# Parameter rows on ScalarE's queue, all of x loaded ahead of the embedding product, first six weight loads behind x

## The chip, the cores and the metric

The kernel runs on one core of one Trainium2 chip. The core has five engines that run side by side and wait for one another through semaphores: TensorE (PE in the profile; its weight loads are PEld), VectorE (DVE), ScalarE (ACT), GpSimd (POOL) and SyncE (SP). Data moves between HBM and the on-chip memory by DMA, over 16 DMA engines. The metric is the device time of one execution in microseconds (us); lower is better.

## The reference

One decoder layer over 1024 tokens of width 1024, all in float32:

```
u  = rms_norm(x, ln_g)
z  = u @ w_in                       # 1024 x 7168, split into val, glu, gate, q, f, i, g
y_conv = conformer_conv_branch(val, glu, gate, ...)   # GLU, causal conv of width 31, norm, swish, projection
y_hgrn = hgrn2_branch(q, f, i, g, ...)                # gated linear recurrence, 8 heads
h  = x + concat(y_conv, y_hgrn) @ w_out
pe = p @ w_pp                       # p is 1024 x 256
h  = h + sigmoid(rms_norm(h, pe_norm_g) @ w_pg) * pe
out = rms_norm(h, final_g)
```

Nine small parameter tables (the convolution's 31 taps, biases, norm gains, two rows of logits) have one value per channel.

## The kernel before

Every matrix product is made of three float32r products of a high and a low part (hi·hi, hi·lo, lo·hi). The part `split` makes them: ScalarE copies the high part, VectorE subtracts it from the source for the low part.

The program is written with a scheduler that keeps, for each engine, one fixed order of instructions; an engine works strictly down its list, and an instruction that has to wait holds up all behind it. The order follows the order of the code, bent by `tc.high_priority(n)`, which lets a block be placed as if it stood n instructions earlier. DMAs are issued by the engine whose queue they stand in (`nc.sync` is SP, `nc.scalar` is ACT), in the same list as that engine's other work. All DMAs together share eight completion semaphores in turn (DMAHW0 to DMAHW7), so a DMA may have to wait until the one that used its semaphore before it has landed.

The prologue, lines 139 to 238, is what the change touches:

- Lines 143 to 154: p is loaded in two halves (`prows`), transposed on TensorE into PSUM (`pT`), and split (`pTh`, `pTl`). Line 155: `w_pp` is loaded and split (`wpp0h`, `wpp1h`, `wpp0l`, `wpp1l`).
- `scale_x` (lines 157 to 169): for each of four token blocks, x is loaded (`xt`), ScalarE sums the squares (`jk`, `ss`), GpSimd makes the reciprocal root (`rx`), VectorE scales the block.
- `load_params` (lines 81 to 106): nine DMAs bring the parameter rows into one tile `prow` of 40 rows; TensorE transposes it (`pt`), VectorE copies it into `par`; `lbt` and `oml` follow from two small exponentials (`le`).
- `norm_x` (lines 171 to 183): TensorE transposes the scaled x (`ut`, four PSUM banks, tag "t"), ScalarE and VectorE make `uh` and `ul` with the gain from `par`.
- Lines 225 to 237, the embedding product: 16 tiles `pe` of six matmuls each (PSUM tag "z", four banks), each copied out by ScalarE (`pes`, two buffers) and stored to HBM (`pe_d`).

After it come the products `z` of `u` and 56 column blocks of `w_in` (`product`, lines 240 to 250, called by `ztile` and `values`), each with a weight load of 512 KB, `wz` or `wv`, split into a high and a low part. The three raw, three high and three low weight buffers are shared with `w_pp`. In the kernel before, the second half of x is loaded only after the embedding product in the code (line 238), and all weight loads of `ztile` and `values` have a priority of 2000, which takes the first of them ahead of x.

Of the kernel before, what the change touches and what calls it, by code (L numbers as in the profile page):

```python
# [20 lines left out]
TAPS = 31  # L21
# [11 lines left out]
R_CB, R_CG, R_CBETA, R_BPW, R_L0, R_L1, R_ON, R_LN, R_PE = range(TAPS, TAPS + 9)  # L33
# [4 lines left out]
def trunk_kernel(ctx: ExitStack, tc: tile.TileContext, x, p, ln_g, w_in, conv_w, conv_b,  # L38
                 cnorm_g, cnorm_b, w_pw2, b_pw2, lb_logits, onorm_g, w_out, pe_norm_g,
                 w_pg, w_pp, final_g, out):  # L40
    nc = tc.nc
# [36 lines left out]
    lbt = cst.tile([P, G], F32, name="lbt")  # L78
    oml = cst.tile([P, G], F32, name="oml")

    def load_params(work):
        rows = work.tile([NR, D], F32, name="prow")
        nc.sync.dma_start(rows[0:TAPS, :], conv_w[0])
        for r, ap in ((R_CB, conv_b), (R_CG, cnorm_g), (R_CBETA, cnorm_b), (R_BPW, b_pw2),
                      (R_ON, onorm_g), (R_LN, ln_g), (R_PE, pe_norm_g)):
            nc.sync.dma_start(rows[r:r + 1, :], ap)
        nc.sync.dma_start(rows[R_L0:R_L0 + 2, :], lb_logits)
        pt = bank("t", "pt")
        for g in range(G):
            nc.tensor.transpose(pt[:, g * NR:(g + 1) * NR], rows[:, g * P:(g + 1) * P],  # L90
                                ident[:NR, :NR])
        nc.vector.tensor_copy(par, pt[:, :G * NR].rearrange("p (g r) -> p g r", r=NR))

        l0, l1 = par[:, :, R_L0], par[:, :, R_L1]
        mx = cst.tile([P, G], F32, name="lmx")
        e0 = cst.tile([P, G], F32, name="le0")
        e1 = cst.tile([P, G], F32, name="le1")
        nc.vector.tensor_tensor(mx, l0, l1, op=ALU.max)
        nc.vector.tensor_tensor(e0, l0, mx, op=ALU.subtract)
        nc.vector.tensor_tensor(e1, l1, mx, op=ALU.subtract)  # L100
        nc.scalar.activation(e0, e0, AF.Exp)
        nc.scalar.activation(e1, e1, AF.Exp)
        nc.vector.tensor_tensor(e1, e0, e1, op=ALU.add)
        nc.vector.reciprocal(e1, e1)
        nc.vector.tensor_tensor(lbt, e0, e1, op=ALU.mult)
        nc.vector.tensor_scalar(oml, lbt, -1.0, 1.0, op0=ALU.mult, op1=ALU.add)
# [32 lines left out]
    with tc.tile_pool(name="st", bufs=1) as st:  # L139

        KP = p.shape[1] // P
        pT = []
        for hf in range(2):
            rows = st.tile([P, 4, KP * P], F32, tag="prows", bufs=2, name=f"prows{hf}")
            nc.sync.dma_start(rows, p[hf * H:(hf + 1) * H, :].rearrange("(b p) c -> p b c", p=P))
            for k in range(KP):
                pt = bank("t", f"pT{hf}_{k}")
# [6 lines left out]
                pT.append((hi, lo))  # L154
        wpp = [prep(w_pp[k * P:(k + 1) * P, :], [P, D], f"wpp{k}") for k in range(KP)]

        def scale_x(hf):
            xs = []
            for b in range(4):
                tb = hf * 4 + b  # L160
                xt = st.tile([P, D], F32, tag="xt", bufs=8, name=f"xt{tb}")
                nc.sync.dma_start(xt, x[tb * P:(tb + 1) * P, :])
                jk = st.tile([P, D], F32, tag="jk", bufs=2, name=f"jk{tb}")
                ss = sml.tile([P, 1], F32, tag="ss", bufs=4, name=f"ss{tb}")
                sumsq(xt, ss, jk)
                r = rstd_of(ss, 1, 1.0 / D, f"rx{tb}")
                nc.vector.tensor_scalar(xt, xt, r, None, op0=ALU.mult)
                xs.append(xt)
            return xs
# [12 lines left out]
                                               uh[hf][k].bitcast(F32),  # L182
                                               op0=ALU.mult, op1=ALU.subtract)

        xs = scale_x(0)
        load_params(st)


        ones = st.tile([P, 4 * 48], F32, name="ones")
# [28 lines left out]
        for l in (2, 8):  # L218
# [2 lines left out]
            for j0, cnt in ((0, 3), (3, 2), (5, 1)):  # L221
                block_mask(mv[:, :, j0:j0 + cnt, :], 0, 4 * l, l, l)
            masks[l] = own_block(l, mf)
        norm_x(0, xs)
        for tb in range(G):
            pet = st.tile([P, D], F32, tag="pet", bufs=2, name=f"pes{tb}")
            c = slice(tb % 4 * P, (tb % 4 + 1) * P)
            for j in range(2):
                z = bank("z", f"pe{tb}_{j}")
                for k in range(KP):  # L230
                    hi, lo = pT[tb // 4 * KP + k]
# [3 lines left out]
                    mm(z, lhsT=lo[:, c], rhs=wh, start=False, stop=k == KP - 1)  # L235
                nc.scalar.activation(halves(pet)[j], z, AF.Copy)
            nc.sync.dma_start(pe_d[tb * P:(tb + 1) * P, :], pet)
        norm_x(1, scale_x(1))

    def product(wh, wl, mh, ml, tag, name):  # L240

# [7 lines left out]
            res.append(z)  # L249
        return res  # L250

    def ztile(idx):
        with tc.high_priority(2000):
            wh, wl = prep(colblock(w_in, idx * P), [P, G, P], f"wz{idx}")
        return product(wh, wl, uh, ul, "z", f"z{idx}")

    def values(idx, vt):

        with tc.high_priority(2000):
            ws = [prep(w_in[j * H:(j + 1) * H, idx * P:(idx + 2) * P]  # L260
                       .rearrange("(k p) c -> p k c", p=P), [P, 4, 2 * P], f"wv{idx}_{j}")
                  for j in range(2)]
        for tb in range(G):
            hf, c = tb // 4, slice(tb % 4 * P, (tb % 4 + 1) * P)
            z = bank("z", f"v{idx}_{tb}")[:, :2 * P]
            for k in range(G):
                wh, wl = (w[:, k % 4, :] for w in ws[k // 4])
                mm(z, lhsT=uh[hf][k][:, c], rhs=wh, start=k == 0, stop=False)  # L268
                mm(z, lhsT=uh[hf][k][:, c], rhs=wl, start=False, stop=False)  # L269
                mm(z, lhsT=ul[hf][k][:, c], rhs=wh, start=False, stop=k == G - 1)  # L270
            nc.scalar.activation(vt[:, tb, :], z, AF.Copy)  # L271
# [520 lines left out]
    for tb in range(G):  # L792
# [26 lines left out]
        r = rstd_of(ss, 1, 1.0 / D, f"rf{tb}")  # L819
# [35 lines left out]
```

## Time and profile before

| | us |
|---|---|
| median of 3 runs | 1146.06 (1145.93 to 1148.94) |
| the profiled execution, its own time | 1143.71 |
| span of its trace, first to last instruction | 1141.7 |
| TensorE busy in the span | 1111.5 (97%) |
| VectorE busy | 821.5 (72%) |
| ScalarE busy | 461.4 (40%) |
| GpSimd busy | 73.2 (6%) |
| 16 DMA engines, mean | 99 GB/s |

The profiled execution's own time is 2.0 us over its span. Busy time of TensorE is modelled, so what tells more is where it is idle and which clock it was granted. In the 40 slices of the page TensorE is 9 tenths busy or more in all but the first and the last; the first slice is the prologue.

### The profile page before, as it was taken

What the parts mean: (1) busy time and instruction counts of PE and PEld (TensorE: products, weight loads), DVE (VectorE), ACT (ScalarE), POOL (GpSimd) and SP (SyncE); (2) the same over time, 40 slices, a digit from 0 to 9 for tenths busy, and PEclk for the clock granted to TensorE, in tenths of its full rate; (3) what the DMA queues carried; (4) which work ended last, traced back from release to release, by engine and by line L of the source; (5) the groups of instructions that cost most, each with busy time, mean ns of one, the idle gap of its engine ahead of it and who ended that gap; (6) DMA issues with size and microseconds to landing.
All of it is one profiled execution on the core that took longest, in us unless ns stands there. A gap on an engine that the chain in (4) does not pass through costs nothing.

```text
span 1141.7 us, 17945 instructions
## 1 busy us (share of the span) xinstructions
PE 1111.5 (97%) x7312; PEld 927.8 (81%) x7312; DVE 821.5 (72%) x1313; ACT 461.4 (40%) x867; POOL 73.2 (6%) x107
## 2 busy tenths in 40 slices
PE   6999999999999999999999999999999999999997
PEld 4888978889878789788798788887677887787886
DVE  3659579998499996599994896356876744667544
ACT  4832254253354442343532532444334311237533
POOL 3100001001001010001010010000000000001200
PEclk9999999999999999999999999999999999999999
DMA  7611120211111112111111113136486754432222
GB/s 250 235 37 56 37 66 29 74 53 42 56 57 56 56 38 75 56 38 56 57 57 56 57 43 106 59 118 222 148 276 203 229 180 161 155 114 91 93 92 74
DMA packets 96851, 112.98 MB, mean 99 GB/s; under 512 B 4186, under 2 KB 74842, under 8 KB 96770
## 3 DMA queue, kind: packets, MB, share of 16 engines
q1 hardware_dynamic: 96770, 111.85, 29.9%
q8 instruction: 57, 0.93, 0.3%
q14 instruction: 24, 0.20, 0.1%
HBM read 82.48 MB, written 29.36 MB: 98 GB/s over the span
## 4 chain that ended last, share of the span: by engine, by line
PE 80%; DVE 9%; DMA 7%; ACT 2%; issue 1%; SPq 0%; POOL 0%; POOLq 0%; ACTq 0%; DVEq 0%
PE z L246 14%; PE z L247 14%; PE z L248 13%; DVE y L457 4%; PE v L270 3%; PE v L269 3%; PE v L268 3%; PE pg L808 3%; PE pg L806 3%; PE pg L807 3%; PE pw L729 2%; PE pw L730 2%; PE pw L728 2%; DMA wpg<-in_w_pg_dram 1%; PE sc L300 1%; PE o L432 1%
## 5 line engine op out<-in xcount | busy, mean ns | idle before, releaser
L457 DVE SCALAR_TENSOR_TENSOR y<-vpad,par,y 128x1024 f32<-128x1024 f32 x232 | 288.8, 1278 | 1.1
L806 PE MATMUL pg<-gh,hh 128*128 128x512 f32 (+1 forms) x136 | 51.5, 379 | 2.0 <-ACT hh L755 2.0
L807 PE MATMUL pg<-gl,hh 128*128 128x512 f32 (+1 forms) x136 | 51.6, 379 | 0.0
L808 PE MATMUL pg<-gh,hl 128*128 128x512 f32 (+1 forms) x136 | 51.5, 379 | 0.0
L524 DVE TENSOR_TENSOR vpad<-z,gl 128x512 f32<-128x512 f32 x16 | 11.0, 690 | 42.7 <-PE z L248 42.7
L268 PE MATMUL v<-wv_0h,uh 128*128 128x256 f32 x128 | 36.7, 287 | 0.0
L270 PE MATMUL v<-wv_0h,ul 128*128 128x256 f32 x128 | 36.5, 285 | 0.0
L269 PE MATMUL v<-wv_0l,uh 128*128 128x256 f32 x128 | 36.5, 285 | 0.0
L270 PE MATMUL v<-wv_1h,ul 128*128 128x256 f32 x128 | 36.2, 283 | 0.0
L268 PE MATMUL v<-wv_1h,uh 128*128 128x256 f32 x128 | 36.2, 283 | 0.0
L269 PE MATMUL v<-wv_1l,uh 128*128 128x256 f32 x128 | 36.2, 283 | 0.0
L271 ACT ACTIVATE vt<-v 128x256 f32<-128x256 f32 x32 | 12.2, 382 | 59.0 <-PE v L270 59.0
L812 DVE TENSOR_TENSOR gt<-gt,pet 128x512 f32<-128x512 f32 (+1 forms) x17 | 11.2, 661 | 32.8 <-ACT gt L811 32.8
L113 POOL TENSOR_SCALAR ro<-sso 128x8 f32<-128x8 f32 x8 | 8.4, 1054 | 389.5 <-ACT on L134 389.5
L480 DVE TENSOR_SCALAR y<-yt,mv,ry 128x128 f32<-128x128 f32 x64 | 23.5, 403 | 13.1 <-POOL ry L114 13.1
L806 PEld LDWEIGHTS pg<-gh,hh 128*128 128x128 f32 x136 | 25.6, 188 | 6.7 <-ACT hh L755 2.2
L442 ACT ACTIVATE on<-o,ro 128x128 f32<-128x128 f32 x64 | 18.6, 388 | 29.6 <-POOL ro L114 29.6
L807 PEld LDWEIGHTS pg<-gl,hh 128*128 128x128 f32 x136 | 25.6, 188 | 4.6
L808 PEld LDWEIGHTS pg<-gh,hl 128*128 128x128 f32 x136 | 25.6, 188 | 4.5
L732 DVE SCALAR_TENSOR_TENSOR sgr<-pw,par,sgr 128x512 f32<-128x512 f32 x16 | 11.9, 748 | 23.9 <-PE pw L730 22.5
L488 ACT ACTIVATE yc<-yn,par 128x512 f32<-128x512 f32 x16 | 12.5, 778 | 37.0 <-PE yn L487 36.9
L134 ACT ACTIVATE on<-o 128x128 f32<-128x128 f32 x64 | 16.9, 278 | 23.2 <-PE up L414 18.9
(700 smaller groups left out, 3540.8 us busy)
## 6 DMA issues: line engine op xcount, KB each, us to landing
wz<-in_w_in_dram SPq DMA_DIRECT2D x48, 512.0 KB
xt<-in_x_dram SPq DMA_DIRECT2D x8, 512.0 KB
pe_d<-pes SPq DMA_DIRECT2D x8, 512.0 KB
wv<-in_w_in_dram SPq DMA_DIRECT2D x8, 512.0 KB
yc_d<-yc SPq DMA_DIRECT2D x8, 512.0 KB
yh_d<-sgT SPq DMA_DIRECT2D x8, 512.0 KB
sg_d<-sgc SPq DMA_DIRECT2D x8, 512.0 KB
woab<-in_w_out_dram SPq DMA_DIRECT2D x8, 512.0 KB
```

The source lines that it names most:

```text
L246: mm(z, lhsT=wh[:, k, :], rhs=mh[hf][k], start=k == 0, stop=False)
L247: mm(z, lhsT=wh[:, k, :], rhs=ml[hf][k], start=False, stop=False)
L248: mm(z, lhsT=wl[:, k, :], rhs=mh[hf][k], start=False, stop=k == G - 1)
L268: mm(z, lhsT=uh[hf][k][:, c], rhs=wh, start=k == 0, stop=False)
L269: mm(z, lhsT=uh[hf][k][:, c], rhs=wl, start=False, stop=False)
L270: mm(z, lhsT=ul[hf][k][:, c], rhs=wh, start=False, stop=k == G - 1)
L457: nc.vector.scalar_tensor_tensor(y[j % 2], vp[:, j:j + T], pcol(g, j), y[j % 2], op0=ALU.mult, op1=ALU.add)
L480: nc.vector.tensor_scalar(yt[:, cc * P:(cc + 1) * P], pts[hf][:, c * P:(c + 1) * P], mv[:, cc, 0:1], r[:, cc:cc + 1], op0=ALU.subtract, op ...
L728: mm(z, lhsT=wh, rhs=ych[hf][k], start=k == 0, stop=False)
L806: mm(z, lhsT=hh[k][:, c], rhs=gh[j][k][:, o:o + w], start=k == 0, stop=False)
L807: mm(z, lhsT=hh[k][:, c], rhs=gl_[j][k][:, o:o + w], start=False, stop=False)
L808: mm(z, lhsT=hl[k][:, c], rhs=gh[j][k][:, o:o + w], start=False, stop=k == G - 1)
```

## The change

`load_params` is cut in two: `load_rows` issues the nine DMAs, now from ScalarE's queue and called first of all, and `load_params` does the rest. Both halves of x are loaded and scaled before the parameters are worked on and before the embedding product. A helper `ahead` gives the first six calls of `ztile` and `values` (seven weight loads, since `values` makes two) a priority of 150 in place of 2000; all later ones keep 2000.

```
-    def load_params(work):
+    def load_rows(work):
         rows = work.tile([NR, D], F32, name="prow")
-        nc.sync.dma_start(rows[0:TAPS, :], conv_w[0])
+        nc.scalar.dma_start(rows[0:TAPS, :], conv_w[0])
         for r, ap in ((R_CB, conv_b), (R_CG, cnorm_g), (R_CBETA, cnorm_b), (R_BPW, b_pw2),
                       (R_ON, onorm_g), (R_LN, ln_g), (R_PE, pe_norm_g)):
-            nc.sync.dma_start(rows[r:r + 1, :], ap)
-        nc.sync.dma_start(rows[R_L0:R_L0 + 2, :], lb_logits)
+            nc.scalar.dma_start(rows[r:r + 1, :], ap)
+        nc.scalar.dma_start(rows[R_L0:R_L0 + 2, :], lb_logits)
+        return rows
+
+    def load_params(rows):
         pt = bank("t", "pt")
...
         KP = p.shape[1] // P
+        prow = load_rows(st)
         pT = []
...
-        xs = scale_x(0)
-        load_params(st)
+        xs = [scale_x(0), scale_x(1)]
+        load_params(prow)
...
-        norm_x(0, xs)
+        norm_x(0, xs[0])
...
-        norm_x(1, scale_x(1))
+        norm_x(1, xs[1])
...
+    taken = []
+
+    def ahead():
+
+        taken.append(0)
+        return tc.high_priority(2000 if len(taken) > 6 else 150)
+
     def ztile(idx):
-        with tc.high_priority(2000):
+        with ahead():
...
     def values(idx, vt):
 
-        with tc.high_priority(2000):
+        with ahead():
```

The order of the instructions changes only in the prologue; from the first `z` tiles on, every engine's list is the same as before. In the pieces below, `[waits ...]` names the semaphores that an instruction waits for; the figure behind a semaphore's name means nothing here, and the numbers in the tile names are the program's own.

ScalarE before, from its first instruction: it loads its function table and then copies the high parts as the DMAs land.

```order
L118 ACT_TABLE_LOAD
L118 ACTIVATE wpp0h<-wpp_153 128x1024 [waits DMAHW2_49]
L118 ACTIVATE pTh_0_120<-pT_0_115 128x512 [waits PE_49]
L118 ACTIVATE wpp1h<-wpp_159 128x1024 [waits DMAHW3_49]
L118 ACTIVATE wz8h<-wz_611 128x1024 [waits DMAHW4_49]
```

ScalarE in the changed kernel, from its first instruction.

```order
L83 DMA prow<-in_conv_w_dram 31x1024
L86 DMA prow<-in_conv_b_dram 1x1024
L86 DMA prow<-in_cnorm_g_dram 1x1024
L86 DMA prow<-in_cnorm_b_dram 1x1024
L86 DMA prow<-in_b_pw_dram 1x1024 [waits DMAHW0_49]
L86 DMA prow<-in_onorm_g_dram 1x1024 [waits DMAHW2_49]
L86 DMA prow<-in_ln_g_dram 1x1024 [waits DMAHW4_49]
L86 DMA prow<-in_pe_norm_g_dram 1x1024 [waits DMAHW6_49]
L87 DMA prow<-in_lb_logits_dram 2x1024 [waits DMAHW0_49]
L121 ACT_TABLE_LOAD
L121 ACTIVATE pTh_0_130<-pT_0_125 128x512 [waits PE_49]
```

Nine DMA issues now stand ahead of all of ScalarE's work. DMAHW0 was given to `conv_w` and then to `b_pw`, so the fifth issue waits for the landing of the first, and the ninth for the landing of the fifth.

SP before, from its fifth DMA: the first weight block goes ahead of x, three more between the first two blocks of x and the next, and the parameter rows behind these.

```order
L124 DMA wz_611<-in_w_in_dram 128x8x128
L162 DMA xt_165<-in_x_dram 128x1024
L162 DMA xt_174<-in_x_dram 128x1024
L124 DMA wz_669<-in_w_in_dram 128x8x128 [waits DMAHW2_49,DVE_49]
L124 DMA wz_727<-in_w_in_dram 128x8x128 [waits DMAHW3_49,DMAHW0_49,DVE_49]
L124 DMA wz_788<-in_w_in_dram 128x8x128 [waits DMAHW4_49,DMAHW1_49,DVE_49]
L162 DMA xt_183<-in_x_dram 128x1024
L162 DMA xt_192<-in_x_dram 128x1024
L83 DMA prow<-in_conv_w_dram 31x1024
```

SP in the changed kernel, from its fifth DMA.

```order
L166 DMA xt_175<-in_x_dram 128x1024 [waits DMAHW1_49]
L166 DMA xt_184<-in_x_dram 128x1024 [waits DMAHW3_49]
L166 DMA xt_193<-in_x_dram 128x1024 [waits DMAHW5_49]
L166 DMA xt_202<-in_x_dram 128x1024 [waits DMAHW7_49]
L166 DMA xt_211<-in_x_dram 128x1024 [waits DMAHW1_49]
L166 DMA xt_220<-in_x_dram 128x1024 [waits DMAHW2_49]
L166 DMA xt_229<-in_x_dram 128x1024 [waits DMAHW3_49]
L166 DMA xt_238<-in_x_dram 128x1024 [waits DMAHW4_49]
L127 DMA wz_611<-in_w_in_dram 128x8x128 [waits DMAHW5_49]
L127 DMA wz_669<-in_w_in_dram 128x8x128 [waits DMAHW6_49,DVE_49]
L127 DMA wz_727<-in_w_in_dram 128x8x128 [waits DMAHW7_49,DVE_49]
L241 DMA pe_d<-pes_376 128x1024 [waits Activation_49]
```

All eight blocks of x stand directly behind p and `w_pp`, and the weight blocks and the stores of `pes` behind x.

ScalarE before, where the first `uh` is made: four blocks of x have been squared (`jk`) and four tiles of the embedding product copied out (`pes`) ahead of it.

```order
L236 ACTIVATE pes_358<-pe_1_367 128x512 [waits PE_49]
L134 ACTIVATE jk_185,ss_186<-xt_183 128x1024 [waits DMAHW2_49,Activation_49]
L134 ACTIVATE jk_194,ss_195<-xt_192 128x1024 [waits DMAHW3_49,Activation_49]
L236 ACTIVATE pes_376<-pe_0_377 128x512 [waits DMAHW5_49,PE_49,Activation_49]
L101 ACTIVATE le_222<-le_222 128x8 [waits DVE_49]
L102 ACTIVATE le_223<-le_223 128x8 [waits DVE_49]
L180 ACTIVATE uh_0_273<-ut_0_268,par 128x512 [waits PE_49]
```

ScalarE in the changed kernel, at the same place.

```order
L137 ACTIVATE jk_231,ss_232<-xt_229 128x1024 [waits DMAHW3_49,Activation_49,Pool_49]
L137 ACTIVATE jk_240,ss_241<-xt_238 128x1024 [waits DMAHW4_49,Activation_49,Pool_49]
L104 ACTIVATE le_258<-le_258 128x8 [waits DVE_49]
L105 ACTIVATE le_259<-le_259 128x8 [waits DVE_49]
L184 ACTIVATE uh_0_309<-ut_0_304,par 128x512 [waits PE_49]
L240 ACTIVATE pes_376<-pe_0_377 128x512
L184 ACTIVATE uh_1_318<-ut_1_313,par 128x512 [waits PE_49]
```

All eight blocks of x are squared before the first `uh`, and the first copy of an embedding tile (`pes_376`) stands behind it. On TensorE four embedding tiles now stand ahead of that point, and the fifth, `pe_0_413`, needs the bank that `pes_376` empties; behind it stand the other eleven tiles.

## Rows read from the trace of the kernel before

**Rows 1.** The page's chain that ended last: shares of the span by engine

```profile
PE 80%; DVE 9%; DMA 7%; ACT 2%; issue 1%; SPq 0%; POOL 0%; POOLq 0%; ACTq 0%; DVEq 0%
```

**Rows 2.** Busy time by stage; the first line names the columns

```profile
core 0: us, PE busy (x) PEld busy (x) DVE busy (x) ACT busy (x) POOL busy (x), PEclk, DMA share, GB/s
0.00:24.40 24.40, 17.28 (x64) 13.29 (x64) 10.96 (x19) 12.84 (x20) 11.38 (x30) 0.93 0.83 262
24.40:27.64 3.24, 0.00 (x0) 0.03 (x1) 0.11 (x1) 0.00 (x0) 0.00 (x0) 0.82 0.28 115
27.64:32.30 4.66, 4.66 (x25) 4.58 (x26) 2.93 (x10) 3.24 (x8) 0.00 (x0) 0.50 1.00 362
32.30:45.50 13.20, 13.20 (x66) 10.93 (x66) 7.81 (x11) 12.15 (x23) 4.75 (x10) 0.96 0.72 276
45.50:48.30 2.80, 1.74 (x17) 1.50 (x16) 2.80 (x3) 2.80 (x5) 0.82 (x4) 1.00 0.16 60
48.30:1141.70 1093.40, 1074.61 (x7147) 897.50 (x7145) 796.88 (x1273) 430.37 (x814) 56.28 (x64) 1.00 0.28 92
```

**Rows 3.** The chain in order of time: start us, us, what

```profile
15.68 10.04 DMA prow<-in_conv_w_dram
...
25.73 1.45 DMA prow<-in_lb_logits_dram
```

**Rows 4.** SP's DMA issues of the second half of x: start us, us

```profile
26.95 1.88 SPq L162 DMA_DIRECT2D xt<-in_x_dram  x2
...
33.56 1.50 SPq L162 DMA_DIRECT2D xt<-in_x_dram  x2
```

**Rows 5.** Three short stretches by engine, columns as in rows 2

```profile
3.50:5.00 1.50, 0.00 (x0) 0.00 (x0) 0.02 (x1) 0.00 (x0) 1.50 (x3) 1.00 1.09 384
6.00:7.50 1.50, 1.50 (x9) 1.50 (x9) 0.08 (x1) 0.00 (x0) 1.50 (x6) 1.00 1.02 404
21.00:25.00 4.00, 3.37 (x15) 2.44 (x13) 1.50 (x2) 1.49 (x4) 1.72 (x4) 1.00 0.06 26
```

**Rows 6.** The DMA view of 21 to 25 us: pieces moved

```profile
DMA packets 25, 0.10 MB, mean 26 GB/s; under 512 B 0, under 2 KB 0, under 8 KB 25
```

**Rows 7.** TensorE in order of time: start us, us, line, what, idle before

```profile
5.12 3.64 PE L149 MATMUL pT<-ident,prows 128*128 128x128 f32 x16 [5.12 <-DMA prows<-in_p_dram]
...
37.19 0.39 PE L233 MATMUL pe<-wpp0h,pTh 128*128 128x512 f32 x1
...
45.14 0.39 PE L235 MATMUL pe<-wpp1h,pTl 128*128 128x512 f32 x1
...
46.93 1.64 PE L176 MATMUL ut<-ident,xt 128*128 128x128 f32 x13 [1.06 <-DVE xt L167]
48.32 0.48 PE L246 MATMUL z<-uh,wz8h 128*128 128x512 f32 x1
```

**Rows 8.** ScalarE in order of time, columns as in rows 7

```profile
0.78 1.28 ACT L118 ACT_TABLE_LOAD   x1 [0.78 <-PEq L839]
7.78 1.06 ACT L118 ACTIVATE wpp0h<-wpp 128x1024 fp32r<-128x1024 f32 x1 [5.71 <-DMA wpp<-in_w_pp_dram]
...
10.86 1.06 ACT L118 ACTIVATE wz8h<-wz 128x1024 fp32r<-128x1024 f32 x1 [0.60 <-DMA wz<-in_w_in_dram]
11.82 1.55 ACT L118 ACTIVATE pTh<-pT 128x512 fp32r<-128x512 f32 x3
13.26 1.07 ACT L134 ACTIVATE jk<-xt 128x1024 f32<-128x1024 f32 x1
...
14.30 1.06 ACT L134 ACTIVATE jk<-xt 128x1024 f32<-128x1024 f32 x1
...
29.66 0.21 ACT L101 ACTIVATE le<-le 128x8 f32<-128x8 f32 x1 [0.28 <-DVE le L99]
...
29.87 0.67 ACT L180 ACTIVATE uh<-ut,par 128x512 fp32r<-128x512 f32 x1
30.45 0.59 ACT L236 ACTIVATE pes<-pe 128x512 f32<-128x512 f32 x1
```

## The prediction

> **What bounds the kernel now.** I read the chain that ended last first: four fifths of it are TensorE [rows 1], so only time in which TensorE waits or runs slowly can be won. The busy time by stage shows where that is [rows 2]. After 48.30 us TensorE is busy for 1074.61 of 1093.40 us, and from there on the change leaves the order on every engine as it was. All that can be won lies before. There the table shows three losses: from 24.40 to 27.64 us TensorE does nothing (3.24 us); from 27.64 to 32.30 us it is busy throughout but at a granted clock of 0.50, the lower of its two levels (1.2 of 2.4 GHz), after that idle stretch, and so loses about half of 4.66 us, 2.33; and from 45.50 to 48.30 us it is busy for 1.74 of 2.80, where it waits 1.06 us for the last scaled block of x [rows 7]. Together that is 6.6 us, 0.6% of the time.
>
> The chain says what the first wait is for: `conv_w`, the 31 rows of taps, issued at 15.68 us behind weights and x, takes 10.04 us, and `lb_logits`, whose issue waits for that landing, another 1.45 [rows 3]. The second half of x goes out only from 26.95 to 35.06 us, behind them on SP's list [rows 4], which is why its last block is late at 46.93. The change goes straight at both: the rows go out first, from another queue, and x no longer waits for them.
>
> **What conv_w costs wherever it runs.** From 21 to 25 us nearly nothing but `conv_w` moves: DMA share 0.06, one sixteenth, 26 GB/s [rows 5], 25 pieces of 4 KB in 4.00 us [rows 6]. So it runs on one of the 16 DMA engines, at 0.16 us a piece, and its 31 pieces take 4.96 us of that engine. When all sixteen work, 404 GB/s are moved [rows 5], 25 GB/s each, so this one engine is as fast as it ever is. Every 512 KB block that is spread over the sixteen also has its sixteenth on that engine, and has landed only when that part has.
>
> The Trainium skill bears on this. "DMA: Bandwidth & Descriptors", in its section on why a DMA increments its semaphore by 16, has a DMA from SP or ACT use the largest number of engines up to 16 that divides the row count, on the lowest-numbered ones; for 31 rows that is one, and the trace agrees (share 0.06). Its section "Issuing engines are not separate DMA queues" says that a DMA issued from ScalarE runs on the same 16 engines and only saves issue time, and the section on queues has each engine alternate between the queues it has work for. That speaks against this change: by it the sum below stands, and without it x would land 6.2 us sooner (my second rival). No run here shows two queues at once.
>
> **When x is there.** I add up the work of that one engine up to the last block of x, in the new order. The two halves of p, 1.05 MB at 384 GB/s, take 2.73 us [rows 5]; `w_pp`, 1.05 MB at 404 GB/s, 2.60; the eight blocks of x, 4.19 MB, 10.38; `conv_w` 4.96; one 4 KB piece of each of the eight other parameter loads 1.28. The sum is 21.95 us. Start-up and landing come out of before: the first half of p (1.37 us of transfer) has released TensorE at 5.12 us [rows 7], so the fixed part is 3.75 us; as a test, 3.75 + 2.73 + 1.30 gives 7.78 for the first half of `w_pp`, and ScalarE is released for it at 7.78 [rows 8]. The last block of x thus lands at 25.7 us; before, it was not even issued then [rows 4].
>
> **What waits for it.** In the new order ScalarE squares all eight blocks before the first `uh`. From the landing at 25.70: one square 1.04 us (14.30 − 13.26), the two exponentials 0.21, `uh` 0.58, then `pes` 0.59 [rows 8], so the bank that the fifth embedding tile needs is free at 28.1 us. TensorE cannot go on until then: eleven of its tiles stand behind. From 28.2 us it has 72 matmuls at 0.227 us (37.19 to 45.14, 36 of them, 35 steps) and 32 transposes at 0.107 (1.39 us for 13) before the first `z` [rows 7], 16.3 + 3.4 = 19.8 us. The first `z` starts at 48.0 us at the full clock. Before it started at 48.32. What the change wins in the waits it gives back by doing, after 28 us, twelve of sixteen tiles that were half done by then: before, eight were finished at 24.4 (the 64 instructions of the first stage are 16 transposes and 48 matmuls [rows 2]).
>
> **The clock.** TensorE comes to 28.2 us out of a stretch in which its transposes follow the blocks of x as they are scaled, and then a pause. After the pause of 3.24 us before, it ran at 0.50 for 4.66 us; after the one of 1.06 us it kept 1.00 [rows 2]. So the restart costs between nothing and 2.33 us. The pause here should be between these two, after a stretch half idle; I take 1.2. A pause of `ul` behind weight splits on VectorE after the embedding tiles could add a few tenths, which I leave in the range.
>
> The sum: first `z` at 49.2 us, 0.9 later than before, from −0.3 to +2.0. On the profiled execution's own time, 1143.71 us, that is 1144.6; the median of the runs shown is 2.35 us above it, and on that I give 1147.0.
>
> **The other parts.** ScalarE's nine issues and waits stand ahead of its first copy. `conv_w` takes turns on its engine with the 1 KB pieces of p (64 of them in 2.73 us, 0.043 each): 3.75 + 4.96 + 31 × 0.043 gives a landing at 10.0 us. After it ScalarE has one round trip of `b_pw` (1.45, as `lb_logits` took when it was alone [rows 3]), the table load 1.28, four `pTh` at 0.48 (11.82 to 13.26 for three), two `w_pp` copies at 0.96 (10.86 to 11.82), eight squares at 1.04, then 0.21, 0.58 and 0.59 [rows 8]: 16.3 us, so 26.3 us. That is 1.8 us before the bound by x; this slack hides the whole move onto ScalarE, and is gone if `conv_w` lands after 11.8 us. For p the new neighbour is not free either, TensorE should start near 10 us instead of 5.12, but it is not what the restart at 28.2 waits for.
>
> The first weight blocks: `wz8` was split at 10.86 and is needed at 49. Three blocks behind x are 1.57 MB, 5.7 us at the 276 GB/s of the stage from 32.30 [rows 2], so there by 32 us; the next two high parts wait for buffers that `w_pp` holds to the end of the embedding product, as before. Cost nothing; if that cover went, 1.9 us for one block. The stores of `pes` queue behind them on SP, with two buffers and 2.7 us of TensorE work for each pair of tiles; nothing, or some tenths. The split of `load_params` itself changes no instruction.
>
> **Rivals.** First, on the slower side: ScalarE's own list becomes the bound. If the two queues share the engine byte for byte, `conv_w` has half of it and lands at 3.75 + 9.92 = 13.7 us. With the 16.3 us behind it the bank is free at 30.0, `z` starts at 51.0, 2.7 us late. If `b_pw`, which must go out only after that landing, also waits behind what SP has queued (up to four blocks of 1.30 us, 5.2, in place of 1.45), it is 6.4 late. The middle is 4.5: 1150.6. It decides from 11.8 us on for the landing plus anything over 1.45 in the round trip. For it: both are loads in a crowd, which before never shows for the second. Against: p's pieces are four times smaller than `conv_w`'s.
>
> Second: the two queues do not hinder each other, so x lands at 25.70 − 6.24 = 19.5 us. Then ScalarE's list sets the end, with `conv_w` landing at 8.7 and the bank free at 25.0 us; `z` starts between 44.8 and 47.1 us, middle 2.3 us early: 1143.8. Against: the one engine is already at its rate alone.
>
> Third: the change does all that it says, and the 6.6 us of the three losses go: 1139.4. It needs the first `uh` by some 21 us, which neither ScalarE's list nor x allows by the rows.
>
> **How the numbers follow.** A difference under 0.3%, 3.4 us, can't be told from no change. My forecast has 0.50, nearly all of it within that (0.48), 0.02 slower. The first rival has 0.30; its place from 2.7 to 6.4 us puts 0.20 beyond 3.4 and 0.10 within. The second has 0.14, 0.13 of it within and 0.01 faster. The third has 0.06, 0.05 faster. So faster 0.06, within 0.72, slower 0.22. The forecast's own range is 1145.8 to 1148.1; the range given reaches down over the second rival, to 1143.2, and up to the middle of the first, 1150.6. The third and the upper part of the first are left out.
>
> **What would show it.** TensorE's first transposes near 10 us; ScalarE's table load not before 10 us; the last square of x near 26, the first `uh` about a microsecond behind it; a pause of TensorE before the fifth embedding tile and a granted clock below 1.00 in the stage behind it; the first `z` near 49 us. If the last square starts well before 25 us, the shared engine is wrong. If the squares follow one another without a wait for x and end at 28 us or later, it is the first rival. If TensorE starts at 5 us as before and `conv_w` has still landed by 9, the second.

## The result and the profile after

| | kernel before | changed kernel |
|---|---|---|
| median of 7 runs each, us | 1145.93 (1143.48 to 1148.94) | 1154.21 (1150.89 to 1155.38) |
| the profiled execution, its own time | 1143.71 | 1150.89 |
| span of its trace | 1141.7 | 1149.2 |
| start of the first `z` | 48.32 | 57.23 |

The ratio is 1.0074, 95% interval 1.0059 to 1.0089: slower, by 8.5 us (6.8 to 10.2). The forecast was 1147.0, from 1143.2 to 1150.6. The first `z` starts 8.91 us later than before, and from there to the end the two traces need nearly the same, 1091.97 and 1093.40 us. So everything lost is lost in the prologue.

Busy time of the changed kernel by stage, cut at the events of TensorE; this answers to [rows 2], and the columns are the same.

```profile
0.00:20.20 20.20, 4.59 (x24) 4.20 (x24) 5.29 (x13) 5.02 (x7) 7.74 (x22) 1.00 0.70 222
20.20:30.03 9.83, 9.25 (x42) 6.84 (x41) 6.22 (x12) 9.83 (x22) 7.49 (x13) 1.00 1.05 333
30.03:30.99 0.96, 0.96 (x4) 0.48 (x3) 0.69 (x1) 0.96 (x3) 0.88 (x2) 1.00 0.90 228
30.99:36.24 5.25, 0.00 (x0) 0.00 (x1) 4.09 (x6) 2.64 (x5) 3.75 (x6) 0.71 0.29 111
36.24:40.25 4.01, 4.01 (x17) 3.41 (x17) 3.98 (x8) 1.85 (x4) 0.00 (x0) 0.52 0.23 89
40.25:55.57 15.32, 15.32 (x73) 12.62 (x71) 2.20 (x4) 8.04 (x14) 0.25 (x2) 1.00 0.59 214
55.57:57.23 1.66, 1.66 (x17) 1.66 (x16) 1.05 (x1) 1.66 (x4) 0.00 (x0) 1.00 0.10 40
57.23:1149.20 1091.97, 1072.25 (x7147) 895.12 (x7145) 796.59 (x1274) 431.31 (x815) 56.28 (x64) 1.00 0.29 92
```

In the first 20.20 us TensorE does 4.59 us of work, where before it did 17.28 in 24.40. From 30.99 to 36.24 it stands still, and behind that it runs 4.01 us at 0.52, about the lower of its two levels (1.2 of 2.4 GHz). Two thirds of the embedding product, which was half done at 24.4 us before, are then done from 40 to 55 us. Within the first 20 us TensorE does wait for DMAs, as the next rows show; in the pause the DMA engines are busy for a share of only 0.29, the last column but one.

TensorE of the changed kernel in order of time (start us, us, line, what, idle before), answering to [rows 7].

```profile
11.64 3.65 PE L153 MATMUL pT<-ident,prows 128*128 128x128 f32 x16 [11.64 <-DMA prows<-in_p_dram]
19.25 1.04 PE L93 MATMUL pt<-ident,prow 40*128 40x40 f32 x8 [3.96 <-DMA prow<-in_lb_logits_dram]
...
30.03 0.50 PE L237 MATMUL pe<-wpp0h,pTh 128*128 128x512 f32 x1
...
36.24 1.12 PE L180 MATMUL ut<-ident,xt 128*128 128x128 f32 x4 [5.25 <-DVE ul L185]
...
57.23 0.47 PE L250 MATMUL z<-uh,wz8h 128*128 128x512 f32 x1
```

ScalarE in the changed kernel, answering to [rows 8]; ACTq is its queue, whose issues stand in the same list as its work.

```profile
0.78 0.52 ACTq L83 DMA_DIRECT2D prow<-in_conv_w_dram  x1
...
10.55 0.21 ACTq L86 DMA_DIRECT2D prow<-in_b_pw_dram  x1
...
14.89 0.24 ACTq L87 DMA_DIRECT2D prow<-in_lb_logits_dram  x1
15.17 1.28 ACT L121 ACT_TABLE_LOAD   x1 [15.17 <-DMA prow<-in_b_pw_dram]
...
20.29 1.07 ACT L137 ACTIVATE jk<-xt 128x1024 f32<-128x1024 f32 x1
...
27.57 1.05 ACT L137 ACTIVATE jk<-xt 128x1024 f32<-128x1024 f32 x1
...
28.81 0.68 ACT L184 ACTIVATE uh<-ut,par 128x512 fp32r<-128x512 f32 x1
29.38 0.59 ACT L240 ACTIVATE pes<-pe 128x512 f32<-128x512 f32 x1
```

`b_pw` goes out when `conv_w` has landed, at 10.5 us, `lb_logits` when `b_pw` has, 4.3 us later, and only then does ScalarE load its table, at 15.17 in place of 0.78. The eight squares follow one another without a gap from 20.29 to 28.6 us: x is there, ScalarE is late.

SP's issues in the changed kernel: `prows` is p, `xt` all of x.

```profile
0.79 0.98 SPq L149 DMA_DIRECT2D prows<-in_p_dram  x2
1.82 0.97 SPq L127 DMA_DIRECT2D wpp<-in_w_pp_dram  x2
11.52 7.85 SPq L166 DMA_DIRECT2D xt<-in_x_dram  x8
```

The first x block takes the completion semaphore that the first half of p has, and this has landed only at 11.5 us: its 32 pieces on the one engine take turns with the 31 of `conv_w`, so both are done at about the same time, 10.5 and 11.5 us. Busy time of a stretch just before shows the one engine still at work: DMA share 0.08, 28 GB/s, near what `conv_w` alone had [rows 5]. The DMA view of 9.0 to 9.8 us has four pieces of 4 KB from ScalarE's queue and four of 1 KB from SP's, one of each by turns.

```profile
8.60:10.40 1.80, 0.00 (x0) 0.00 (x0) 0.50 (x3) 0.00 (x0) 0.00 (x0) 1.00 0.08 28
```

The chain of the changed kernel's first 60 us, the links just ahead of the pause's end (start us, us, engine, what, line).

```profile
31.48 0.76 POOL rx L116
32.32 0.56 POOL rx L117
32.91 2.55 DVE xt L171
35.52 0.67 DVE ul L185
36.24 1.12 PE ut L180 x4
```

This is what the prediction did not have. The fifth `ut` needs a PSUM bank that the first `uh` and `ul` read. `uh` is made at 28.81, but the first `ul` stands on VectorE's list behind all eight scalings of x, and these come every 1.47 us, although the squares that feed them come every 1.04: the scaling waits for GpSimd's `rx`, and the first operation of the next `rx` (L116) takes as long as the scaling that runs beside it, 0.75 us. VectorE of the changed kernel at the end of that row, columns as for TensorE:

```profile
31.43 0.76 DVE L171 TENSOR_SCALAR xt<-xt,rx 128x1024 f32<-128x1024 f32 x1 [0.72 <-POOL rx L117]
32.91 2.55 DVE L171 TENSOR_SCALAR xt<-xt,rx 128x1024 f32<-128x1024 f32 x1 [0.72 <-POOL rx L117]
...
35.45 0.74 DVE L185 SCALAR_TENSOR_TENSOR ul<-ut,par,uh 128x512 fp32r<-128x512 f32 x1
```

And GpSimd of the changed kernel in the same stretch:

```profile
31.48 0.76 POOL L116 TENSOR_SCALAR rx<-ss 128x1 f32<-128x1 f32 x1
...
32.82 1.84 POOL L289 MEMSET AT<- 128x1024 f32 x2
```

The eighth scaling takes 2.55 us where the others take 0.75; two memsets run on GpSimd beside it. The kernel before has the same pair (first and last line here), and between them the first operation of an `rx` that no scaling runs beside:

```profile
44.18 2.69 DVE L167 TENSOR_SCALAR xt<-xt,rx 128x1024 f32<-128x1024 f32 x1 [0.72 <-POOL rx L114]
...
34.86 0.19 POOL L113 TENSOR_SCALAR rx<-ss 128x1 f32<-128x1 f32 x1 [11.14 <-ACT jk L134]
...
44.09 1.85 POOL L278 MEMSET AT<- 128x1024 f32 x2
```

What the eight scalings ahead of `ul` cost comes mostly from the two engines holding each other up. An estimate from these rows: if they did not, an `rx` would take 0.86 us up to its scaling (34.86 to 35.72 in the kernel before), the scalings would keep up with the squares, and the eighth would end 0.86 + 0.75 us after the last square is summed at 28.7, at 30.3 us in place of 35.46. By this estimate nearly the whole pause is contention: some 1.8 us the memsets, which an experiment below tests, and some 3.3 the turns with `rx`, which none does.

The time of the first `z` adds up: the fifth embedding tile at 30.03 (28.2 forecast), 19.8 us of work at the full clock, 5.25 of pause, and 57.23 − 30.03 − 19.8 − 5.25 = 2.15 us as the remainder, for the lower clock (1.2 forecast); 4.01 us at 0.52 alone lose 1.9.

### The profile page after: what moved, and what is told of

Its sections match the earlier page's. It is cut to its first block, busy times and chain, and to the rows that moved or that the text cites. A ratio compares the mean times of both kernels' runs of the same rounds, so it can differ in the third digit from the quotient of the medians.

```text
span 1149.2 us, 17945 instructions
## 1 busy us (share of the span) xinstructions
PE 1108.0 (96%) x7312; PEld 924.3 (80%) x7312; DVE 820.1 (71%) x1313; ACT 461.3 (40%) x867; POOL 76.4 (7%) x107
## 4 chain that ended last, share of the span: by engine, by line
PE 80%; DVE 10%; DMA 4%; ACT 2%; issue 1%; POOL 0%; SPq 0%; POOLq 0%; ACTq 0%; DVEq 0%
PE z L250 14%; PE z L251 13%; PE z L252 13%; DVE y L468 4%; PE v L280 3%; PE v L281 3%; PE v L279 3%; PE pg L819 3%; PE pg L818 3%; PE pg L817 3%; PE pw L740 2%; PE pw L741 2%; PE pw L739 2%; DMA wpg<-in_w_pg_dram 1%; PE sc L311 1%; PE o L443 1%
## 5 line engine op out<-in xcount | busy, mean ns | idle before, releaser
L116 POOL TENSOR_SCALAR ro<-sso 128x8 f32<-128x8 f32 x8 | 8.4, 1055 | 389.6 <-ACT on L137 389.6
```

## The experiments

Theory L: ScalarE's list starts late because it holds the DMA issues, and `ul` is late because it stands behind eight scalings on VectorE's; the first `z` carries the whole difference in time. The rivals: x, landing late on the one engine (X); the weight blocks behind x (W); and, for the end of the pause, a cause of the 2.55 us other than GpSimd's memsets (M).

One table for all; "time" is the ratio less one, times the median of the kernel before that was measured beside it on the same chip (1145.0 to 1146.0), with its 95% interval. The starts are from one profile each.

| kernel | first `z`, us | against 48.32 | time against before, us |
|---|---|---|---|
| changed kernel | 57.23 | +8.9 | +8.5 (6.8 to 10.2) |
| rows from SP | 52.72 | +4.4 | +3.6 (2.2 to 4.8) |
| second half scaled late | 51.41 | +3.1 | +3.1 (0.9 to 5.3) |
| taps as 16 + 15 | 52.39 | +4.1 | +4.6 (3.0 to 6.2) |
| both of these | 46.97 | −1.4 | −1.5 (−3.0 to 0.1) |
| memsets on VectorE | 55.24 | +6.9 | +7.1 (5.4 to 8.9) |
| before + weights behind x | 40.49 | −7.8 | −5.7 (−7.9 to −3.4) |
| before + taps as 16 + 15 | 44.02 | −4.3 | −4.4 (−6.3 to −2.4) |
| x, then rows, from SP | 45.80 | −2.5 | −2.5 (−4.0 to −1.1) |
| the same, memsets on VectorE | 44.51 | −3.8 | −8.0 (−10.2 to −5.8) |
| the same again | 44.58 | −3.7 | −5.0 (−6.9 to −3.2) |
| rows between the halves of x | 48.39 | +0.1 | −0.9 (−2.5 to 0.7) |
| the same, memsets on VectorE | 47.43 | −0.9 | −1.5 (−3.2 to 0.1) |

Twelve of the thirteen rows (all but the first of the two same kernels) have the move of the first `z` inside the interval of the time or at its edge: that start is the measure of this change, within intervals 2.6 to 4.5 us wide.

**The rows from SP, all else as changed.** All nine issues move, as the first does here.

```
-        nc.scalar.dma_start(rows[0:TAPS, :], conv_w[0])
+        nc.sync.dma_start(rows[0:TAPS, :], conv_w[0])
...
```

> The changed kernel with its nine parameter rows issued from SP again, ahead of p; x is still loaded ahead of the embedding product. The scheduler then also puts the first four `ul` after five to eight scalings of x on VectorE's list, one in between each, and the first `pes` after two squares on ScalarE's. Theory L (two lists: ScalarE begins its work 15.2 us late because its issues wait for conv_w's landing, and `ul` waits 5.25 us behind eight scalings): ScalarE's table load starts near 8 us, the pause of TensorE before `ut` shrinks from 5.25 us to under 2, the first z starts at 49 to 52 us in place of 57.2, the time is 5 to 7 us below the changed kernel. Rival X (the DMA engine that carries conv_w sets when x is there, whoever issues it): the last x block lands at 25 to 27 us as before, the first z stays at 55 to 57, the time within 2 us of the changed kernel.

ScalarE loaded its table at 0.78 (8 expected), but the first `z` came at 52.72, just outside the 49 to 52, and the time 4.9 us below the changed kernel (5 to 7 expected). SP in this kernel:

```profile
0.79 0.35 SPq L83 DMA_DIRECT2D prow<-in_conv_w_dram  x1
...
7.88 0.23 SPq L87 DMA_DIRECT2D prow<-in_lb_logits_dram  x1
8.16 0.95 SPq L149 DMA_DIRECT2D prows<-in_p_dram  x2
```

The wait for `conv_w` has gone with its issue to SP, where p stands behind it, and TensorE began at 12.52 us. This also gives `conv_w` alone: released 7.1 us after its issue, against 9.8 beside p. Half of the loss is gone, so X as "whoever issues it" falls; but neither queue takes this wait for nothing. The longest pause that is left, a little over the 2 us expected, is again behind the eighth scaling (2.62 us beside the memsets):

```profile
37.21 1.12 PE L180 MATMUL ut<-ident,xt 128*128 128x128 f32 x4 [2.12 <-DVE ul L185]
```

**The second half of x loaded early, scaled late.**

```
-        xs = [scale_x(0), scale_x(1)]
+        xs = [load_x(0), load_x(1)]
+        scale_x(0, xs[0])
...
-        norm_x(1, xs[1])
+        norm_x(1, scale_x(1, xs[1]))
```

`load_x` holds the four loads of a half, `scale_x` its squares, `rx` and scalings.

> The changed kernel with one thing moved: all of x is loaded as early as there, but the second half is squared and scaled only where the kernel before did it, behind the embedding product. The row loads stay on ScalarE. Theory L: `ul` of the first block stands behind four scalings in place of eight, so the pause of 5.25 us before the fifth `ut` goes (under 1 us is left), ScalarE reaches the first `uh` some 4 squares (4.2 us) sooner, at about 24.6 us, but still not before its table load at 15; the first z starts at 50.5 to 53 us in place of 57.2, the time 4.5 to 6.5 us below the changed kernel, and 2 to 4 above the kernel before. Rival X (the landing of x, on the shared DMA engine): nothing of the loads has changed, so x lands at 26.9 as now, and z stays within 1.5 us of 57.2. Rival W (the weight blocks behind x are what is late): z also stays near 57.

TensorE in this kernel, the pause that is left and the first `z`:

```profile
31.96 0.66 PE L184 MATMUL ut<-ident,xt 128*128 128x128 f32 x4 [0.77 <-DVE ul L189]
...
51.41 0.47 PE L255 MATMUL z<-uh,wz8h 128*128 128x512 f32 x1
```

The pause falls from 5.25 to 0.77 us, the lower clock with it, and the first `z` comes 5.8 us sooner with the same loads (ScalarE's table load still at 15.13). X falls, and W as the cause of the 5.25 us. What is left is W's: the split of the first weight block stands ahead of the first `uh` and `ul`, ScalarE waited 1.58 us for that block to land, and the first `uh` came at 29.89, not at 24.6.

**The taps as 16 and 15 rows.**

```
-        nc.scalar.dma_start(rows[0:TAPS, :], conv_w[0])
+        nc.scalar.dma_start(rows[0:16, :], conv_w[0, 0:16])
+        nc.scalar.dma_start(rows[16:TAPS, :], conv_w[0, 16:TAPS])
```

> The changed kernel with conv_w loaded as 16 and 15 rows in two DMAs, so that its pieces no longer go to one DMA engine; all lists otherwise as in the changed kernel. Theory L: conv_w lands by 4 us in place of 10.5, so ScalarE's table load starts at 7 to 9 us in place of 15.2 and TensorE starts near 5 us in place of 11.6; x is issued from about 5 us. The eight scalings stay ahead of `ul` on VectorE, so a pause of 3 to 5 us before the fifth `ut` stays, but earlier by what x is earlier (5 to 6 us). First z at 50.5 to 53 us, the time 4 to 6.5 us below the changed kernel. Rival A (the alternation of two queues on one engine is not what delayed the landing; the loads are slow at the start for another reason): table load still after 12 us, z after 55.

ScalarE in this kernel, its last issue and its table load:

```profile
10.28 0.24 ACTq L88 DMA_DIRECT2D prow<-in_lb_logits_dram  x1
10.55 1.28 ACT L122 ACT_TABLE_LOAD   x1 [10.55 <-DMA prow<-in_b_pw_dram]
```

TensorE in the same kernel:

```profile
31.59 1.01 PE L181 MATMUL ut<-ident,xt 128*128 128x128 f32 x4 [4.89 <-DVE ul L186]
...
52.39 0.47 PE L251 MATMUL z<-uh,wz8h 128*128 128x512 f32 x1
```

TensorE began at 5.82 us, the table load came 4.6 us sooner (later than the 7 to 9 expected: the issues now wait one by one for turns that loads of p, `w_pp` and x hold), and the pause stayed, earlier by as much; the time is 3.9 us below the changed kernel (4 to 6.5 expected). Rival A of that text falls.

**Both together.**

> The changed kernel with both repairs: the second half of x is scaled late, and conv_w goes out as 16 and 15 rows; the rows are still issued from ScalarE, x is still loaded ahead. Alone, the first brought the first z from 57.2 to 51.4 us, the second ScalarE's table load from 15.2 to 10.5. Theory L (two separate causes, one on ScalarE's list and one on VectorE's): they add, ScalarE's table load is at 10.5, TensorE's pause before `ut` under 1 us, the first z at 46 to 48 us, and the time within 0.3% of the kernel before, whose z starts at 48.3. Rival B (one cause under two names): no better than the better of the two, z at 50 or later and the time still 2 us or more above before.

They add: no pause before `ut`, the first `z` at 46.97 us (46.6 if the two gains are summed), the time that of the kernel before. Two separate causes.

**The memsets on VectorE.**

```
-        nc.gpsimd.memset(AT[i], 0.0)
+        nc.vector.memset(AT[i], 0.0)
...
-    nc.gpsimd.memset(AB, 0.0)
+    nc.vector.memset(AB, 0.0)
```

> The changed kernel with the three memsets of AT and AB on VectorE in place of GpSimd; there they stand behind all `ul`. They start now at 32.8 us, beside the eighth scaling of x, which takes 2.55 us where the seven others take 0.75. Theory L with contention between GpSimd and VectorE: the eighth scaling takes 0.75 us, the first `ul` comes 1.8 us sooner, the pause of TensorE before `ut` is 3.4 us in place of 5.25, the first z starts at 55 to 55.7 us in place of 57.2; the time is up to 2 us below the changed kernel, less what the memsets cost on VectorE. Rival M (the eighth scaling is long for another reason): it stays above 2 us and z at 57.

VectorE's eighth scaling in this kernel:

```profile
33.13 0.75 DVE L171 TENSOR_SCALAR xt<-xt,rx 128x1024 f32<-128x1024 f32 x1 [0.71 <-POOL rx L117]
```

TensorE's pause behind it:

```profile
34.67 1.11 PE L180 MATMUL ut<-ident,xt 128*128 128x128 f32 x4 [3.32 <-DVE ul L185]
```

0.75 in place of 2.55, the pause 1.93 us shorter, the first `z` 2.0 sooner; the time difference to the changed kernel is inside the two intervals. Rival M falls; the contention of the memsets is shown. The 3.32 us that stay are what the estimate above gives for the turns with `rx`; no run took these away while all eight scalings stood ahead, so this part is not shown.

**The third part of the change alone, on the kernel before.** The helper `ahead` and its two calls, as in the diff above, and nothing else.

> The kernel before with the third part of the change alone: the first six weight calls have the lower priority, so their loads stand behind the first four blocks of x and the parameter rows on SP; conv_w is then issued four blocks (some 5 us) sooner. Theory L (the weight order is harmless, and conv_w's landing is what TensorE waits for in the kernel before): conv_w lands near 19 to 21 us in place of 25.7, the wait of 3.24 us before `ut` and the lower clock behind it go, the first z at 43 to 46 us in place of 48.3, the time 2 to 5 us below the kernel before. Rival W (the later weight loads, or second-half x loads that now stand behind stores of `pes` and weight loads, cost time): z at 50 or later, or a pause of over 1 us between the first z tiles; the time at or above the kernel before, and most of the 8.3 us of the change is here.

Its first `z`, and the pauses of TensorE behind it:

```profile
40.49 0.48 PE L246 MATMUL z<-uh,wz8h 128*128 128x512 f32 x1
...
42.18 0.66 PE L176 MATMUL ut<-ident,xt 128*128 128x128 f32 x4 [0.74 <-DVE xt L167]
...
48.19 0.66 PE L176 MATMUL ut<-ident,xt 128*128 128x128 f32 x4 [1.03 <-DVE xt L167]
```

`conv_w` goes out at 4.88 us in place of 15.68, `pt` is made at 23.58 without a wait, and the first `z` is 7.8 us sooner (2.3 to 5.3 expected). Of this 5.7 stay: eight transposes, 0.9 us, now stand behind the first `z`, and TensorE waits 0.74 and 1.03 us for later blocks of x, which stand behind stores on SP; the second of these waits also has the memsets in it (an eighth scaling of 2.68 us). So W's pause of over 1 us is there, but not its price: W falls, and this part of the change is a gain by itself, 0.5% (0.3 to 0.7).

**The taps as 16 and 15 rows in the kernel before.** The edit is that of the third experiment, on SP.

> The kernel before with one thing changed: the 31 rows of conv_w go out as two DMAs of 16 and 15 rows in place of one, all orders as before. Theory N (before, conv_w lands 10.04 us after its issue because its 31 pieces run one after another on one DMA engine): with the pieces over 16 and 15 engines the landing comes 4 to 5 us sooner, at 20.5 to 22 us, lb_logits by 23.5; the wait of 3.24 us before `pt` and `ut` falls under 1 us, the lower clock behind it goes, the first z starts at 43 to 45.5 us in place of 48.32, and the time is 3 to 5 us below the kernel before. Rival Q (conv_w is late because it stands behind weights and x in its queue, however it is spread): landing after 24 us, first z within 1 us of 48.3, time the same.

`lb_logits`, which went out at 25.73 us [rows 3], goes out at 22.39; `pt` starts at 24.26 without a wait, and the first `z` at 44.02. Theory N holds, 4.4 us (2.4 to 6.3) for one line. The Trainium skill, "DMA: Bandwidth & Descriptors", in its section on why a DMA increments its semaphore by 16, gives 16 rows sixteen engines; this run agrees as far as the landing goes.

**x, then the rows, from SP; ScalarE free.** The late scaling, the split taps, and:

```
-        prow = load_rows(st)
...
         xs = [load_x(0), load_x(1)]
+        prow = load_rows(st)
         scale_x(0, xs[0])
```

`load_rows` issues from SP here.

> What the theory says the change wanted: SP issues p, w_pp, all eight blocks of x, then the rows (conv_w as 16 and 15); the second half of x is scaled where the code of before has it; the first six weight calls keep the lower priority of the change. ScalarE has no DMA to issue. Theory L: x lands by 20 us, conv_w by 22, `pt` is made by 25, TensorE has its embedding tiles to do from 9 to 25 us and waits less than 1.5 us from there to the first z, which starts at 40 to 42.5 us; and since all of x is scaled by then, the waits of the weights-only version behind the first z do not come; the time is 6 to 10 us below the kernel before and 2 to 5 below the weights-only version (1141.2). Rival W (with all of x and the rows ahead, the first weight blocks are late, or the eight scalings ahead of `ul` hold TensorE up again): a pause of 2 us or more before `ut` or the first z, z after 44, and the time at or above 1141.

The expectation failed, its rival W held. VectorE in this kernel:

```profile
24.32 2.61 DVE L176 TENSOR_SCALAR xt<-xt,rx 128x1024 f32<-128x1024 f32 x1 [0.71 <-POOL rx L118]
26.86 0.47 DVE L96 COPY par<-pt 128x320 f32<-128x320 f32 x1
```

The first `z` came at 45.80, not at 40 to 42.5. With x loaded so early, the scheduler put all eight scalings ahead of the copy of `par`, and TensorE waited 2.57 us for it, `pt` having been made at 22.67. The same trap as in the change, one link further on. With the memsets moved:

> The version with p, w_pp, all of x and then the rows on SP, and beside it the three memsets moved from GpSimd to VectorE, where they stand behind all `ul`. There the first z started at 45.80 us, not at 40 to 42.5, because the copy of `par` stood behind eight scalings on VectorE, the last of them 2.61 us beside the memsets. Theory L with contention: the eighth scaling takes 0.75 us, `par` is copied 1.85 us sooner (25 us in place of 26.86), TensorE's pause of 2.57 us falls to 0.7, the lower clock behind it is shorter or gone, the first z starts at 42.5 to 44 us, the time 2 to 3.5 us below that version's 1143.2. Rival M: the eighth scaling stays over 2 us, z within 0.5 us of 45.8.

The eighth scaling took 0.75 us, `par` was copied at 25.89, the pause was 0.72, another of 1.36 before the next `ut` stayed, and the first `z` came at 44.51: 1.3 sooner, where 1.8 to 3.3 were expected. Against the kernel before the time came out 5.5 us lower still, more than the start can explain, so it was run again:

> The same kernel once more: p, w_pp, all of x, then the rows on SP, conv_w as 16 and 15 rows, and the memsets on VectorE. Its first z came 3.8 us sooner than in the kernel before (44.51 against 48.32 us), yet its median was 7.6 us below, where in the versions in which all of x was scaled by the first z the time moved by what that start moved, within 2 us. If the first z is the whole of it (theory L), the repeat gives 3 to 6 us below before, near 1140, and the first measurement was low by chance; if something behind the first z is won too, it is again 7 us or more below, 1138 or less.

1141.25, 5.0 us below before, with the first `z` at 44.58: the first figure was low by chance, or most of it. The mean granted clock goes with it: 0.997 in four of the first six executions, in two of these eleven.

**The rows between the two halves of x.** The same version, with `load_rows` between `load_x(0)` and `load_x(1)`.

> The same version with the rows between the two halves of x on SP instead of behind both, memsets on GpSimd as ever. The order on VectorE is then: four scalings, the copy of `par`, and the four later scalings one by one between the first `ul`. Theory L (what counts is how many scalings stand ahead of `par` and of the first `ul`): `par` is copied by 24 us, no pause of TensorE before `ut` over 1 us, the first z at 40 to 42.5 us, the time 3 to 5 us below that version's 1143.2 (1138 to 1140), 6 to 8 below the kernel before. Rival X (with the rows ahead of it, the second half of x lands late and holds up ScalarE's list, and `uh` behind its squares): pauses of 2 us or more, z after 44, the time no better than 1143.

> The rows between the two halves of x, and the memsets on VectorE behind all `ul`. Theory L with contention: as with the memsets on GpSimd, less up to 1.85 us where the last scaling stands ahead of a `ul` that TensorE waits for; first z at 39.5 to 42 us, the lowest time of all versions so far, 1136 to 1140. Rival: the memsets on VectorE delay the low parts of the first weight blocks (they stand ahead of the fourth), and the time is no lower than with the memsets on GpSimd.

Both expectations failed: the first `z` came at 48.39 and 47.43, and both times are those of the kernel before within their intervals. `par` was copied in time (23.48 and 24.28), and yet TensorE paused; here with the memsets on GpSimd:

```profile
26.38 0.66 PE L184 MATMUL ut<-ident,xt 128*128 128x128 f32 x4 [1.04 <-DVE ul L189]
...
28.76 0.66 PE L184 MATMUL ut<-ident,xt 128*128 128x128 f32 x4 [1.72 <-DVE ul L189]
...
30.37 0.97 PE L184 MATMUL ut<-ident,xt 128*128 128x128 f32 x4 [0.96 <-DVE ul L189]
...
33.78 1.11 PE L184 MATMUL ut<-ident,xt 128*128 128x128 f32 x4 [1.16 <-DVE ul L189]
```

One square of 1.05 us now stands between every two `uh`, one scaling between every two `ul`, so the 4.88 us are spread over four pauses instead of one, with the clock at 0.66 on the mean of 30 to 40 us. Rival X's figures for the first `z` and the time came out, but not its cause: the squares between the `uh` did not wait for x. What counts is not only what stands ahead of the first `uh` and `ul`, but also what stands between them up to the last bank that TensorE waits for.

## Why the prediction was wrong

The time came out at 1154.21 us for a forecast of 1147.0, the first `z` at 57.23 for 49.2.

**Where the time lies: right.** All of the difference is ahead of the first `z`.

**conv_w on one engine, in company: right, the figure partly by luck.** It landed at 10.5 us (10.0 forecast), TensorE's first transposes came at 11.64 ("near 10"). But alone it lands at 7.88 us (the rows from SP), where the sum's 3.75 + 4.96 gives 8.7, and the company of p cost 2.7 us for 1.3 in the sum: two errors that partly cancel. Spreading it took 4.6 us off ScalarE's start in the changed kernel and 4.4 us off the time of the kernel before.

**When x is there: not the bound.** The sum of 25.70 took x to be issued behind `w_pp` without a pause. It was issued from 11.52 us, since its turn of the semaphores waited for p. The last square started at 27.57 without a wait for x, so ScalarE's list set the end and not x.

**ScalarE's list: the first rival's mechanism, in part.** Forecast were 10.0 + 16.3 = 26.3, measured 29.97 (the end of the first `pes`): 0.5 for the landing, 2.9 for the round trip of `b_pw`, which took 4.3 us in place of 1.45, and the rest some tenths. The 1.45 was a row of a stretch in which nothing else moved; the rival had given up to 5.2 for it in company. Its sign came true as well: the squares followed one another without a wait for x and ended at 28.6. That is 1.8 us of the miss, and by itself would have given 1149, inside the range.

**What waits for it: the step that failed.** "TensorE cannot go on until then: eleven of its tiles stand behind. From 28.2 us it has 72 matmuls ... and 32 transposes": the text followed the bank that `pes` frees and let everything behind it run without a stop. The fifth `ut` stands among these tiles, and its bank is freed by `ul` on VectorE, where the change had put eight scalings ahead. Only weight splits were thought of there, at "a few tenths"; the scalings were put at nothing. They cost 5.25 us, and with the late scaling 0.77 are left. The rows to price them were in the trace of the kernel before: `rx` and the scalings that take turns, and the scaling of 2.69 us beside the memsets at 44.18. The same rows correct the prediction's third loss. The last block of x was late at 46.93 not because it went out late (its square, at 41.66, did not wait for it), but because its scaling took 1.9 us too long. No rival had any of this.

**The clock: priced for a pause that did not come.** The 1.2 us were for a pause before the fifth embedding tile. TensorE came to that tile without one and started it at 30.03 at a clock of 1.00. The lower clock came behind the pause for `ul`: 4.01 us at 0.52 after an idle stretch of 5.25, as 4.66 at 0.50 after 3.24 before [rows 2], and 2.15 us in all. That the sum had a term for it is luck.

49.2 + 1.8 + 5.25 + 0.95 = 57.2, which is the first `z`. **The weight blocks**, costed at nothing, cost nothing in the changed kernel; that alone they would win 5.7 us the text did not see, since in the changed kernel the rows had left SP's list already.

Four versions beat both kernels, with the whole of their intervals below 1: the weights behind x alone (1141.22, ratio 0.995, 0.9931 to 0.997), the split taps alone (1139.84, 0.9962, 0.9945 to 0.9979), x before the rows (1143.17, 0.9978, 0.9965 to 0.999), and the same with the memsets moved (1141.25 in its second run, 0.9956, 0.994 to 0.9972). Their intervals overlap; which is best stays open, and the first two together were not tried.

## What to carry to other kernels

When loads or work are moved ahead, read the whole list of every engine that the moved work runs on, and for each thing that the bottleneck waits for (here two PSUM banks, one freed by ScalarE, one by VectorE) count what now stands in front of it, and price it with what runs beside it on the other engines. A DMA issue on a compute engine's list brings its wait along: with a completion semaphore still held by an earlier load, the engine stands still until that has landed. A latency read in a quiet stretch is a lower bound for a busy one: 1.45 us here became 4.3.

## What the runs showed of the hardware

- Two queues on one DMA engine share it, piece by piece. `conv_w`, 31 pieces, was released 7.1 us after its issue alone and 9.8 beside p, and the first half of p, with as many pieces there, landed at 11.5 in place of 5.1.
- VectorE and GpSimd hold each other up in these operations. The first operation of `rx` on GpSimd took 0.75 us beside a scaling and 0.19 without one (34.86 us in the kernel before); a scaling took 2.55 beside two memsets of 0.92 and 0.75 without. The Trainium skill, "SBUF — State Buffer", section "SBUF: two separate sides", calls their common port pair an exclusive lock: a GpSimd operation, or one of VectorE that uses both ports, holds it for the whole instruction and blocks the other. The trace agrees: the scaling issued at 32.91 ends 0.80 us after the first two memsets do (the third, of 0.32 us, overlaps with it).
- The split of 31 rows into 16 and 15 is worth 4.4 us (2.4 to 6.3) in a kernel of 1146.
